# A hybrid decoder block: engine order pinned at the first seam of its Strassen MLP, other buffers at the second, one shared sum folded in a chunk earlier

## The chip, the cores and the metric

One core of a Trainium2 chip. The time is the device time of one execution in microseconds (us); the span is the part of it that the profile records, from the first instruction to the last. The engines are TensorE (PE, with its weight loads as PEld), VectorE (DVE), ScalarE (ACT), GpSimd (POOL) and SyncE (SP), which here only issues DMAs. All times of engines are from one profiled execution.

## The reference

One pre-norm layer on 1024 tokens of width 1024, in float32: a mixer (a state-space scan and an attention side by side), then an MLP with a squared ReLU, then a last norm. The change lies in the MLP:

```python
h = h + hybrid_mixer(rmsnorm(h, norm_mix_w), ...)
u = square(relu(rmsnorm(h, norm_mlp_w) @ w_up))      # 1024 x 4096
h = h + u @ w_down                                    # 1024 x 1024
return rmsnorm(h, norm_final_w)
```

## The kernel before

Matmuls have float32 quality by splitting: each operand is a high part, a rounded copy, and a low part, the rest; a product is the sum high x high, high x low and low x high, so three matmuls for each k-tile. `parts(o, src, by)` makes both: ScalarE copies the high part, the engine `by` (mostly VectorE) subtracts it to get the low part.

Both matmuls of the MLP are done by a seven-product Strassen scheme on 2 x 2 blocks. Up-projection: 16 pairs of 256 columns of `w_up`. One product of a pair is 12 matmuls of 512 columns into one bank (`up_mm`). The right operands b11, b21, b22, t1 to t4 (tiles `g_...`, four k-tiles each) are made once from the normalised rows and used by all pairs; the left ones (a11, s1, ...) are made for each pair by `up_split`: a sum on GpSimd, then `parts` (tiles `us_s`, `uo_...`). Results pass a bank a, b or c, go through ReLU and square, are summed by four GpSimd operations to the left operands of the down-projection (tiles `uc`), and are stored to DRAM (`uc_d`) by SyncE. Down-projection: 8 chunks of two pairs, in each 4 slots i (token rows i and i+4 of 128); a slot is seven products of 6 matmuls (`down_mm`), whose results VectorE adds to the rows `h1b`, read back from DRAM. Product a is used twice: its second form, the shared sum, is collected over the chunks in `acc`, and in the last chunk GpSimd adds `acc` to three halves of the rows (line 1546). `down_split` makes the right operands of a pair (tiles `do_...`), `down_in` loads and splits the left ones of a slot (tiles `ui`), two slots ahead. `final` norms and stores a row block.

The first seam is the way from the mixer's output projection (`oproj_jobs`, products `po`) into pairs 0 and 1. From the fourth row block on (`row`, line 1371) work for the MLP is placed after a number of matmuls (`after`): `left` (transposes `nt_l`) makes b11 and b21, `right_turn` and `right_sums` the sums `ta` (in `cc` lies a scaled copy). `norm_row` squares a row block on ScalarE, takes its root on GpSimd (`v_m`), and scales it on VectorE (`hn`). After the last `po`, lines 1387 to 1427 write the two pairs out step by step. The second seam is the way from the last two pairs (`tails`, 14 and 15) into chunk 0.

The order of instructions on each engine is chosen by the framework's scheduler: it takes program order as priority, but lets ready instructions go ahead. An engine whose key stands in `kept` has its instructions pinned in program order; before the change that is TensorE alone ("t") at the first seam, and none later. Buffers have tags with a fixed count (`BUFS`, `PBUFS` for banks); a tile waits until a buffer of its tag is free. On the way through the code: tags d, s, t and v are banks (2, 3, 2, 1); `hT`, `q`, `p`, `w`, `ws`, `v`, `t` and `p0` are SBUF buffers.

Of the kernel before, what the change touches and what calls it, by code (L numbers as in the profile page):

```python
# [45 lines left out]
def tile_hymba_block(  # L46
# [1238 lines left out]
    class Up:  # L1285
# [50 lines left out]
        def p7(self):  # L1336
            self.half = self.t1
            self.third(self.prod("b", "s3", "t3"))

        def p5(self):  # L1340
            self.half = self.t1
            self.third(self.prod("c", "s1", "t1"))

        def p4(self):
            b = self.prod("b", "a22", "t4")
# [5 lines left out]
        def p3(self):  # L1351
            c = self.prod("c", "s4", "b22")
            u2 = self.u2
            ve.tensor_tensor(out=u2, in0=c, in1=u2, op=ALU.add)
# [8 lines left out]
            for j in range(3):  # L1363
                sy.dma_start(out=d[:, :, 2 * j:2 * j + 2, :], in_=self.st[j])
            sy.dma_start(out=d[:, :, 6, :], in_=a22)

    OP = {"p1": "a11", "p2": "a12", "p6": "s2", "p7": "s3", "p5": "s1", "p4": "a22", "p3": "s4"}
    ups = {}
# [18 lines left out]
    for p in range(2):  # L1387
        ups[p] = Up(p, "dts")
    ups[0].p1()
    ups[1].p1()  # L1390
    for k in range(HK):
        right_turn(k, 1)
    for k in range(HK):
        right_sums(k, 1)
        parts(gtile("t2", k), ta[k][:, 1, :], ve)
    ups[0].p2()
# [237 lines left out]
```

## Time and profile before

| | us |
|---|---|
| median of 3 runs (1702.18 to 1708.83) | 1706.76 |
| the profiled execution's own time | 1701.5 |
| its span | 1699.7 |
| TensorE busy | 1614.2 |
| VectorE busy | 1113.4 |
| ScalarE busy | 821.6 |
| GpSimd busy | 803.6 |

The page is read from the engine with the largest share: where TensorE is busy all the time, other engines cost nothing; where it pauses, the bracket of the timeline names what it waited for. A pause also has an after-effect, which shows in the granted clock of a stretch and in longer matmuls behind it. Stages: mixer up to 1011, first seam 1011 to 1085, steady pairs to 1318, second seam to 1404, steady chunks to 1642, last chunk and end to 1699.7.

### The profile page before, as it was taken

What the parts mean: (1) busy time and instruction counts of PE and PEld (TensorE: products, weight loads), DVE (VectorE), ACT (ScalarE), POOL (GpSimd) and SP (SyncE); (2) the same over time, 40 slices, a digit from 0 to 9 for tenths busy, and PEclk for the clock granted to TensorE, in tenths of its full rate; (3) what the DMA queues carried; (4) which work ended last, traced back from release to release, by engine and by line L of the source; (5) the groups of instructions that cost most, each with busy time, mean ns of one, the idle gap of its engine ahead of it and who ended that gap; (6) DMA issues with size and microseconds to landing.
All of it is one profiled execution on the core that took longest, in us unless ns stands there. A gap on an engine that the chain in (4) does not pass through costs nothing.

```text
span 1699.7 us, 23561 instructions
## 1 busy us (share of the span) xinstructions
PE 1614.2 (95%) x7994; PEld 1341.5 (79%) x7994; DVE 1113.4 (66%) x2074; ACT 821.6 (48%) x1778; POOL 803.6 (47%) x873
## 2 busy tenths in 40 slices
PE   7999898899999999999999998999999969999996
PEld 7977687778888888888788876788888758888884
DVE  5666775667777677767874537755555646777754
ACT  4223443435565555555631126555445546666643
POOL 4242452454334334434320122655545678777757
PEclk9999899999999999999999999999999989999998
DMA  5122434431120211111442331354554675454432
GB/s 179 38 54 62 93 89 88 103 77 42 36 48 21 48 37 37 36 33 48 134 145 88 100 112 62 119 173 149 160 162 130 206 241 169 141 160 156 147 99 108
DMA packets 180288, 175.41 MB, mean 103 GB/s; under 512 B 44388, under 2 KB 153144, under 8 KB 180168
## 3 DMA queue, kind: packets, MB, share of 16 engines
q1 hardware_dynamic: 179000, 173.12, 34.9%
q8 instruction: 63, 1.03, 0.3%
q0 software_dynamic: 1024, 0.53, 0.1%
q14 instruction: 57, 0.47, 0.1%
q10 hardware_dynamic: 144, 0.26, 0.0%
HBM read 127.15 MB, written 46.73 MB: 102 GB/s over the span
## 4 chain that ended last, share of the span: by engine, by line
PE 69%; DVE 7%; DMA 7%; POOL 6%; ACT 4%; issue 4%; SPq 0%; POOLq 0%; DVEq 0%; ACTq 0%
PE po L85 9%; PE pj_qk L85 9%; PE pu_b L85 6%; PE pj_v L85 5%; DMA eb<-cum_d 5%; PE pn_a L85 4%; PE pu_c L85 4%; PE pn_b L85 4%; PE pn_c L85 4%; PE pu_a L85 4%; PE s L85 4%; PE o L85 4%; PE tp L85 3%; PE pj_x L85 3%; PE pn_d L85 2%
## 5 line engine op out<-in xcount | busy, mean ns | idle before, releaser
L85 POOL TENSOR_SCALAR p<-p,rs 128x512 f32<-128x512 f32 (+2 forms) x144 | 103.3, 722 | 246.6 <-DVE rs L85 133.5
L85 POOL TENSOR_TENSOR ui<-ui 128x384 fp32r<-128x384 f32 (+1 forms) x128 | 145.9, 1161 | 64.9 <-ACT ui L85 51.2
L85 PE MATMUL po<-wh_o,yy 128*128 128x512 f32 x512 | 163.9, 396 | 1.2 <-DVE k L85 1.2
L85 ACT ACTIVATE p<-s,mx 128x512 f32<-128x512 f32 (+1 forms) x192 | 110.4, 579 | 89.8 <-DVE mx L85 69.6
L85 DVE TENSOR_TENSOR pl<-tp,ph 128x512 fp32r<-128x512 f32 x192 | 106.0, 553 | 38.8 <-ACT ph L85 35.9
L85 ACT CAST ph<-tp 128x512 fp32r<-128x512 f32 x192 | 91.7, 478 | 70.1 <-PE tp L85 67.6
L85 ACT CAST ui<-ui 128x384 fp32r<-128x384 f32 (+1 forms) x128 | 71.5, 566 | 104.2 <-DMA ui<-uc_d 102.6
L85 PEld LDWEIGHTS po<-wh_o,yy 128*128 128x128 f32 x512 | 95.5, 189 | 19.7 <-DVE k L85 1.5
L85 PE MATMUL pj_qk<-hh,wl_qk 128*128 128x512 f32 x256 | 106.4, 416 | 0.0
L85 PE MATMUL pj_qk<-hl,wh_qk 128*128 128x512 f32 x256 | 106.3, 415 | 0.0
L85 PE MATMUL pj_qk<-hh,wh_qk 128*128 128x512 f32 x256 | 103.9, 406 | 0.0
L85 PE MATMUL s<-k,q 68*128 68x512 f32 (+7 forms) x384 | 101.9, 347 | 1.0 <-ACT p L85 0.7
L85 PE MATMUL po<-wl_o,yy 128*128 128x512 f32 x256 | 101.6, 397 | 0.0
L85 PE MATMUL pu_b<-g_t,uo_s 128*128 128x512 f32 x384 | 95.9, 400 | 5.0 <-DVE g_t L85 2.9
L85 PE MATMUL pn_c<-do_t,ui 128*128 128x512 f32 x384 | 97.8, 390 | 0.8 <-DVE h1b L85 0.8
L85 PE MATMUL tp<-ident,p 128*128 128x128 f32 x576 | 95.2, 273 | 1.2 <-POOL p L85 1.2
L85 PEld LDWEIGHTS pu_b<-g_t,uo_s 128*128 128x128 f32 x384 | 73.9, 193 | 22.6 <-DVE g_t L85 4.1
L85 PE MATMUL pz<-wh_z,hh 128*128 128x256 f32 (+1 forms) x256 | 77.4, 302 | 15.0 <-DVE z L85 10.9
L85 PE MATMUL pu_a<-g_b,uo_a 128*128 128x512 f32 x384 | 91.6, 389 | 0.0
L85 PEld LDWEIGHTS tp<-ident,p 128*128 128x128 f32 x576 | 72.7, 140 | 19.9 <-POOL p L85 2.6
L85 PEld LDWEIGHTS s<-k,q 128*128 128x128 f32 (+1 forms) x384 | 70.8, 188 | 20.2 <-ACT p L85 4.8
L85 PEld LDWEIGHTS pn_c<-do_t,ui 128*128 128x128 f32 x384 | 71.9, 188 | 16.6 <-DVE h1b L85 1.6
(290 smaller groups left out, 4520.0 us busy)
## 6 DMA issues: line engine op xcount, KB each, us to landing
uc_d<-uc SPq DMA_DIRECT2D x48, 512.0 KB, 3.2
ws_up<-in_w_up_dram SPq DMA_DIRECT2D x32, 512.0 KB, 3.7
wsd<-in_w_down_dram SPq DMA_DIRECT2D x32, 512.0 KB, 4.1
ui<-uc_d SPq DMA_DIRECT2D x64, 256.0 KB, 2.8
ui<-uc_d SPq DMA_DIRECT2D x64, 192.0 KB, 2.4
eb<-cum_d SPq DMA_DIRECT2D x16, 512.0 KB, 8.7
ws_qk<-in_w_in_dram SPq DMA_DIRECT2D x32, 256.0 KB, 3.4
wso<-in_w_out_dram SPq DMA_DIRECT2D x16, 512.0 KB, 3.4
```

The source lines that it names most:

```text
L85: i = call(*args, **kw)
```

## The change

Seven edits.

- First seam, order. From the fourth row block on GpSimd is pinned; after the last `po`, TensorE, VectorE, ScalarE and GpSimd are all pinned until the third product's matmuls are issued. The products are split in a part for TensorE (`m1` ...) and a part that reads the bank (`r1` ...), and the steps are written out in a new order. TensorE's own order stays.
- First seam, t4. Its high part is made by GpSimd rather than ScalarE, right after its sum, and all twelve operations on it are ahead of the second making of s1 on GpSimd. Two of the four k-tiles of b22 are made later. The transposes of the right side come two matmuls later.
- Second seam, homes. The left operands of slots 0 and 1 go to tag `q` (slot 1 was in `p`), those of slot 2 partly to `p` (were in `ws`); the rows of `h1b` go to `hT`, `q`, `q`, `p` (all were in `q`); in the ring of the right operands two `ws` take the place of two `hT`.
- Second seam, sums. The eight GpSimd sums and eight stores of pairs 14 and 15 are written after the loads for slots 0 and 1, no longer before `down_split`.
- Second seam, splits. The right operands of pairs 0 and 1 are split like all others: ScalarE makes a second copy in a bank (tag v), and VectorE subtracts that.
- Second seam, bank. The second product of slot 0 takes a bank of tag s instead of t.
- Shared sum. `acc` is added to the three halves by GpSimd in chunk seven (c = 6); in the eighth VectorE adds the bank itself to the three halves.

```diff
-                ve.tensor_tensor(out=self.u3, in0=bank, in1=self.half, op=ALU.add)
+                ve.tensor_tensor(out=self.u3, in0=bank, in1=self.t1, op=ALU.add)
...
         if dh == 1 and tt == 3:
+            kept.add("g")
             for p in range(2):
                 up_load(p)
...
             for k in range(HK):
-                after(72 + 5 * k, lambda k=k: (right_turn(k, 0), right_sums(k, 0)))
+                after(74 + 5 * k, lambda k=k: (right_turn(k, 0), right_sums(k, 0)))
...
+    kept.update("tvag")
+    u0, u1 = pair = [Up(p, "dts") for p in range(2)]
...
+    def third_sum(k):
+        tb[k] = sb("t", [P, 512], F32, f"tb{k}_3")
+        ve.scalar_tensor_tensor(
+            out=tb[k], in0=p22[k], scalar=mlpw(k + HK), in1=cc[k][:, 0, :], op0=ALU.mult, op1=ALU.subtract
+        )
+        parts(gtile("t3", k), tb[k], ve)
+
+    def fourth_sum(k):
+        tb[k] = sb("t", [P, 512], F32, f"tb{k}_4")
+        gp.tensor_tensor(out=tb[k], in0=cc[k][:, 1, :], in1=ta[k][:, 1, :], op=ALU.subtract)
+        o = gtile("t4", k)
+        gp.tensor_scalar(out=o[:, 0], in0=tb[k], scalar1=1.0, scalar2=1.0, op0=ALU.mult, op1=ALU.mult)
+        gp.tensor_tensor(out=o[:, 1], in0=tb[k], in1=r32(o[:, 0]), op=ALU.subtract)
+
+    u0.m1()
+    u0.r1()
+    u1.m1()
+    up_split(0, "s3", True)
+    u1.r1()
     for k in range(HK):
-        quarter("b22", k, p22[k], mlpw(k + HK))
...
+        right_turn(k, 1)
+    up_split(1, "s3", True)
+    u0.m2()
+    u1.m2()
     for k in range(HK):
...
+        right_sums(k, 1)
+        parts(gtile("t2", k), ta[k][:, 1, :], ve)
+    u0.r2()
+    u0.m6()
+    u1.m6()
+    third_sum(0)
+    third_sum(1)
+    u1.r2()
+    u0.r6()
+    third_sum(2)
+    third_sum(3)
+    u1.r6()
+    u0.m7()
+    u1.m7()
+    for k in range(HK):
+        fourth_sum(k)
+    for k in range(2):
+        parts(gtile("t1", k), ta[k][:, 0, :], ve)
+        quarter("b22", k, p22[k], mlpw(HK + k))
+    up_split(0, "s1", True)
+    for k in range(2, HK):
+        parts(gtile("t1", k), ta[k][:, 0, :], ve)
+    up_split(1, "s1", True)
+    u0.m5()
+    u1.m5()
+    u0.r7()
+    u1.r7()
+    up_split(0, "a22", True)
+    u0.r5()
+    up_split(1, "a22", True)
+    u1.r5()
+    quarter("b22", 2, p22[2], mlpw(HK + 2))
+    quarter("b22", 3, p22[3], mlpw(HK + 3))
+    u0.m4()
+    u1.m4()
...
+    kept.clear()
+    kept.add("t")
+    u0.r3()
+    u1.r3()
+    u0.sums()
+    u1.sums()
+    kept.clear()
...
-    wring = ["hT"] * 14 + ["w"] * 6 + ["hT"] * 2
-    uring = ["q"] * 4 + ["p"] * 4 + ["ws"] * 2
+    wring = ["hT"] * 14 + ["w"] * 6 + ["ws"] * 2
+    uring = ["q"] * 8 + ["p"] * 2
...
-            if p < CP:
-                parts(o, src[m], ve)
-            else:
...
-                hb = ps("s", f"hb_{m}_{p}")
...
+            hb = ps("v" if p < CP else "s", f"hb_{m}_{p}")
+            ac.copy(hb.bitcast(F32R), src[m])
+            ac.copy(o[:, 0], src[m])
+            ve.tensor_tensor(out=o[:, 1], in0=src[m], in1=hb, op=ALU.subtract)
...
-        bb = ps("t", f"pn_b{nm}")
+        bb = ps("t" if c or i else "s", f"pn_b{nm}")
...
-        else:
+        elif not last:
             read(ba, acc[i])
+        if c == NCH - 2:
+            for dst in (h22, h12, h21):
+                gp.tensor_tensor(out=dst, in0=dst, in1=acc[i], op=ALU.add)
         if last:
             for dst in (h22, h12, h21):
-                gp.tensor_tensor(out=dst, in0=dst, in1=acc[i], op=ALU.add)
+                read(ba, dst)
...
+        if i == 2:
+            for u in tails:
+                u.sums()
         for tt in (i, i + 4):
-            h1[tt] = sb("q", [P, D], F32, f"h1b_{tt}")
+            h1[tt] = sb(("hT", "q", "q", "p")[i], [P, D], F32, f"h1b_{tt}")
```

## Rows read from the trace of the kernel before

**Rows 1.** The page's first part, busy time and its share of the span and the instructions of each engine, over the whole execution.

```profile
PE 1614.2 (95%) x7994; PEld 1341.5 (79%) x7994; DVE 1113.4 (66%) x2074; ACT 821.6 (48%) x1778; POOL 803.6 (47%) x873
```

**Rows 2.** Busy time by stretch (from and to in us, length, then busy time and instructions of PE, PEld, DVE, ACT and POOL, TensorE's granted clock, the share of the DMA engines and GB/s): the steady pairs of the up-projection, then the two 20 us stretches of the second seam.

```profile
1085.00:1300.00 215.00, 215.00 (x951) 178.01 (x950) 124.97 (x148) 110.26 (x183) 115.67 (x82) 1.00 0.50 156
...
1340.00:1360.00 20.00, 17.93 (x80) 14.51 (x78) 15.99 (x20) 13.45 (x25) 13.63 (x10) 1.00 0.87 298
...
1360.00:1380.00 20.00, 8.76 (x36) 6.60 (x36) 10.32 (x16) 10.47 (x20) 15.57 (x13) 0.83 0.50 161
```

**Rows 3.** The timeline of TensorE at the first seam (start, length, engine, line, operation, out<-in, tile and form, count, and in brackets the idle time before it and what ended it).

```profile
1021.84 1.11 PE L85 MATMUL nt_l<-ident,hn 128*128 128x128 f32 x4 [3.90 <-ACT cc L85]
...
1040.48 5.61 PE L85 MATMUL pu_a<-g_b,uo_a 128*128 128x512 f32 x24
...
1061.08 0.50 PE L85 MATMUL pu_b<-g_t,uo_s 128*128 128x512 f32 x1 [2.09 <-ACT g_t L85]
...
1062.34 4.10 PE L85 MATMUL pu_b<-g_t,uo_s 128*128 128x512 f32 x9 [0.76 <-DVE g_t L85]
...
1068.60 5.08 PE L85 MATMUL pu_b<-g_t,uo_s 128*128 128x512 f32 x14 [2.16 <-DVE g_t L85]
...
1073.51 5.62 PE L85 MATMUL pu_c<-g_t,uo_s 128*128 128x512 f32 x24
```

**Rows 4.** The timelines of ScalarE, GpSimd and VectorE (columns as in group 3) in the last microseconds of TensorE's pause before 1021.84.

```profile
1014.17 1.05 ACT L85 ACTIVATE hn<-h 128x1024 f32<-128x1024 f32 x1
...
1016.56 0.19 POOL L85 TENSOR_SCALAR v_m<-ss_m 128x1 f32<-128x1 f32 x1
...
1016.83 1.29 POOL L85 TENSOR_TENSOR us_s<-ws_up 128x512 f32<-128x512 f32 x1
...
1018.08 0.55 POOL L85 TENSOR_TENSOR v_m<-v_m,mhalf 128x1 f32<-128x1 f32 x1
...
1018.66 1.74 DVE L85 TENSOR_SCALAR hn<-h,v_m 128x1024 f32<-128x1024 f32 x1 [3.68 <-POOL v_m L85]
```

**Rows 5.** The timelines of GpSimd and VectorE where the operands t2 and t3 are made at the first seam (g_t is their tile, ta and tb their sums).

```profile
1053.62 1.29 POOL L85 TENSOR_TENSOR us_s<-ws_up,ws_up 128x512 f32<-128x512 f32 x1 [4.29 <-DVE uo_s L85]
...
1049.80 0.87 DVE L85 SCALAR_TENSOR_TENSOR ta<-nt_r,prm,ta 128x256 f32<-128x256 f32 x2
...
1053.89 2.78 DVE L85 TENSOR_TENSOR g_t<-ta,g_t 128x512 fp32r<-128x512 f32 x3 [0.35 <-ACT g_t L85]
...
1057.19 1.28 DVE L85 TENSOR_TENSOR g_t<-ta,g_t 128x512 fp32r<-128x512 f32 x2
...
1059.63 2.06 DVE L85 SCALAR_TENSOR_TENSOR tb<-nt_r,prm,cc 128x512 f32<-128x512 f32 x3
...
1067.86 0.68 DVE L85 TENSOR_TENSOR g_t<-tb,g_t 128x512 fp32r<-128x512 f32 x1
```

**Rows 6.** The timeline of TensorE at the second seam; the third and fourth line are the start of slot 1, the last is the start of slot 3.

```profile
1360.57 1.66 PE L85 MATMUL pn_b<-do_t,ui 128*128 128x512 f32 x6 [2.64 <-DVE uu L85]
...
1365.01 1.66 PE L85 MATMUL pn_a<-do_t,ui 128*128 128x512 f32 x6 [1.42 <-DVE h1b L85]
...
1382.08 3.44 PE L85 MATMUL pn_a<-do_b,ui 128*128 128x512 f32 x6 [11.34 <-ACT ui L85]
...
1385.32 2.19 PE L85 MATMUL pn_b<-do_t,ui 128*128 128x512 f32 x6
...
1404.12 1.65 PE L85 MATMUL pn_a<-do_b,ui 128*128 128x512 f32 x6 [0.26 <-ACT acc L85]
```

**Rows 7.** The timelines of GpSimd (first and last sum of the last two pairs), SyncE's queue, ScalarE and VectorE at the second seam.

```profile
1363.62 1.28 POOL L85 TENSOR_TENSOR uc<-uc,uu 128x512 f32<-128x512 f32 x1
...
1375.17 1.26 POOL L85 TENSOR_TENSOR uc<-uc,uc 128x512 f32<-128x512 f32 x1
...
1366.18 10.79 SPq L85 DMA_DIRECT2D uc_d<-uc  x6
...
1377.08 2.85 SPq L85 DMA_DIRECT2D ui<-uc_d  x4
...
1334.51 0.62 ACT L85 CAST do_b<-wsd 128x512 fp32r<-128x512 f32 x1 [3.23 <-DMA wsd<-in_w_down_dram]
...
1363.06 0.58 ACT L85 CAST hb_t<-ds_t 128x512 fp32r<-128x512 f32 x1
...
1363.67 0.69 DVE L85 TENSOR_TENSOR do_t<-ds_t,hb_t 128x512 fp32r<-128x512 f32 x1 [0.35 <-ACT hb_t L85]
```

**Rows 8.** The page's sixth part, DMA issues (count, KB each, median us from issue to landing).

```profile
uc_d<-uc SPq DMA_DIRECT2D x48, 512.0 KB, 3.2
...
ui<-uc_d SPq DMA_DIRECT2D x64, 256.0 KB, 2.8
```

**Rows 9.** Busy time by stretch (columns as in group 2): the four slots of the seventh chunk.

```profile
1604.20:1642.30 38.10, 38.10 (x170) 31.55 (x169) 26.32 (x41) 22.04 (x42) 22.33 (x20) 1.00 0.36 112
```

**Rows 10.** The timelines of TensorE (first and last product of the eighth chunk), GpSimd and VectorE.

```profile
1642.26 1.52 PE L85 MATMUL pn_a<-do_b,ui 128*128 128x512 f32 x6
...
1686.99 1.54 PE L85 MATMUL pn_c<-do_t,ui 128*128 128x512 f32 x6
...
1686.91 3.75 POOL L85 TENSOR_TENSOR h1b<-h1b,acc 128x512 f32<-128x512 f32 x3 [0.73 <-DVE acc L85]
...
1689.47 0.69 DVE L85 TENSOR_TENSOR h1b<-h1b,pn_b 128x512 f32<-128x512 f32 x1 [2.04 <-POOL h1b L85]
```

More of the change, by code (lines that the diff above doesn't have):

```diff
@@ L1334, in third, with m7, r7, m5 @@
                 ac.activation(self.u3, self.u3, AF.Square)
[L1336 to L1345, printed above, removed]
+        def m7(self):
+            self.prod("b", "s3", "t3")
+        def r7(self):
+            self.third(self.bank["b"])
+        def m5(self):
+            self.prod("c", "s1", "t1")
+        def r5(self):
+            self.third(self.bank["c"])
+        def m4(self):
+            self.prod("b", "a22", "t4")
+        def r4(self):
             v = self.view("a12")
-            ve.tensor_tensor(out=v, in0=v3(b), in1=v3(self.t1), op=ALU.add)
+            ve.tensor_tensor(out=v, in0=v3(self.bank["b"]), in1=v3(self.t1), op=ALU.add)
             ac.activation(v, v, AF.Relu)
             ac.activation(v, v, AF.Square)
-        def p3(self):
-            c = self.prod("c", "s4", "b22")
+        def m3(self):
+            self.prod("c", "s4", "b22")
+        def r3(self):
             u2 = self.u2
-            ve.tensor_tensor(out=u2, in0=c, in1=u2, op=ALU.add)
+            ve.tensor_tensor(out=u2, in0=self.bank["c"], in1=u2, op=ALU.add)
             ac.activation(u2, u2, AF.Relu)
             ac.activation(u2, u2, AF.Square)
-            a21, a22, view = v3(u2), v3(self.u3), self.view
+        def sums(self, by=None):
+            a21, a22, view = v3(self.u2), v3(self.u3), self.view
             gp.tensor_tensor(out=view("s3"), in0=view("a11"), in1=a21, op=ALU.subtract)
@@ L1363, in p3, with step @@
             for j in range(3):
[L1364 to L1368, printed above, removed]
+                (by or sy).dma_start(out=d[:, :, 2 * j:2 * j + 2, :], in_=self.st[j])
+            (by or sy).dma_start(out=d[:, :, 6, :], in_=a22)
+        def step(self, n):
+            getattr(self, f"m{n}")()
+            getattr(self, f"r{n}")()
+            if n == 3:
+                self.sums()
+    OP = {1: "a11", 2: "a12", 6: "s2", 7: "s3", 5: "s1", 4: "a22", 3: "s4"}
     def row(tt, dh):
@@ L1386, in tile_hymba_block, with hi, lo @@
     drain()
[L1387 to L1396, printed above, removed]
-    ups[1].p2()
-    ups[0].p6()
-    ups[1].p6()
-    tb = {}
-    for k in range(HK):
+    kept.update("tvag")
+    u0, u1 = pair = [Up(p, "dts") for p in range(2)]
+    tb = {}
+    def hi(m, k, src):
+        ac.copy(gtile(m, k)[:, 0], src)
+    def lo(m, k, src):
+        o = gq[m][k]
+        ve.tensor_tensor(out=o[:, 1], in0=src, in1=r32(o[:, 0]), op=ALU.subtract)
+    def third_sum(k):
         tb[k] = sb("t", [P, 512], F32, f"tb{k}_3")
@@ L1432, in tile_hymba_block @@
         u = Up(p)
-        for m in ("p1", "p6", "p2", "p7", "p5", "p4", "p3"):
-            up_split(p, OP[m])
-            getattr(u, m)()
+        for n in (1, 6, 2, 7, 5, 4, 3):
+            up_split(p, OP[n])
+            u.step(n)
     tails = [Up(p) for p in (NPAIR - 2, NPAIR - 1)]
@@ L1438, in tile_hymba_block @@
         up_load(u.p)
-    for m in ("p1", "p2", "p6", "p5", "p7", "p4", "p3"):
+    for n in (1, 2, 6, 5, 7, 4, 3):
         for u in tails:
-            up_split(u.p, OP[m], True)
+            up_split(u.p, OP[n], True)
         for u in tails:
-            getattr(u, m)()
+            getattr(u, f"m{n}")()
+            getattr(u, f"r{n}")()
     CP = 2
```

47 lines of the change are left out of this document (18 added, 29 removed).

## The prediction, written before the change was run

> **What bounds the kernel now.** I read the busy shares first: TensorE works 95% of the span, the next engine 66% [rows 1], so only stretches in which TensorE pauses can be shortened. Then the table by stretch: in the steady pairs TensorE is busy 215.0 of 215 us at full clock, one matmul of 512 columns every 0.226 us (215/951), in the seventh chunk 38.10 of 38.10 [rows 2, 9]. Nothing is to be had there. So I went through TensorE's timeline for brackets. There are three places.
>
> First seam: a pause of 3.90 us while it waits for ScalarE's copy `cc`, and three of 2.09, 0.76 and 2.16 us ahead of the seventh product, for t3 [rows 3]. Behind them matmuls are stretched: 9 take 4.10 us, 14 take 5.08 us, where 8 and 13 steps of 0.226 and a last 0.39 would be 2.2 and 3.3 [rows 3]. Second seam: 2.64, 1.42 and 11.34 us [rows 6], with a granted clock of 0.83 in that stretch [rows 2]. Last chunk: the first product starts at 1642.26, the last ends at 1686.99 + 6 x 0.226 = 1688.35, so four slots take 46.1 us against 38.1 in the chunk before [rows 9, 10]; then 11.3 us to the span's end at 1699.7.
>
> All sums are made against the profiled execution (1701.5, span 1699.7). The median of the runs is 1706.76, 1.0031 times that; the result is carried over by this ratio.
>
> **First seam, the pause of 3.90.** The chain behind it: ScalarE's square of row block 4 ends at 1014.17 + 1.05 = 1015.2; GpSimd takes it up only at 1016.56, since it is busy with sums of the weights, and puts another (1.29 us) between the two steps of `v_m`; VectorE's scaling of the rows waits until 1018.66 and takes 1.74 us beside GpSimd; the split of b21, in line behind it, and ScalarE's copy follow [rows 4]. These sums, for s2 and s3, are written later than `v_m`; pinned, GpSimd can't hoist them. Then `v_m` goes at 1015.4 and ends 0.27 + 0.55 later, and scaling starts at 1016.3: 2.4 us earlier, and about 1 shorter. TensorE pauses 0.5 instead of 3.9. What the matmuls behind the pause lose I put at 1.2, an estimate from the 1.9 and 1.8 us that the two groups above lose (4.10 against 2.2, 5.08 against 3.3). Together +4.6, bounds 2.4 and 5.1. The sums that are no longer hoisted have until the second operand is split, long after; the two ticks by which the right side's transposes move are two matmuls (0.45 us) of the same TensorE work, nothing.
>
> **First seam, the written order.** TensorE's order doesn't change, so I count what it waits for, from E = 1040.48, the end of `po`; sixteen transposes after m1 end at E + 7.1. Before: the last part of t3 is ready at 1067.86 + 0.68 = E + 28.1, the seventh products end at 1073.51 = E + 33.0, and there is no pause after [rows 3, 5]. Written out, VectorE can't go ahead any more: for each k-tile of t2 it does two sums (0.87 for the two), waits for ScalarE's cast (0.58 [rows 7], and two hand-overs of 0.05), then subtracts (0.60): 2.2 to 2.3, four times, E + 16.4. For t3 a sum of 0.67, a cast, a subtraction: 2.05, four times, and one bank read (0.60) between: E + 25.3. The subtraction has two SBUF operands, and where a GpSimd sum runs it waits: three of them took 2.78 us with a sum of 1.29 that had begun before them, though two alone take 1.28 [rows 5]; a lost 0.9. In the new order GpSimd has twelve operations for t4 in a row from E + 8 on (eight of 1.29 as in the row, four copies that take no more: 13 to 15 us), so seven of the eight subtractions have one beside them. I charge half a sum, 0.6, to each: +4.2, E + 29.5. After that come r6, two k-tiles of t1, two of b22 and s1 (six of about 0.63), and the fifth product starts at E + 33.6 against E + 33.0. A value of -1.0 with the hand-overs. Bounds: no collision is 4.2 earlier (+2.8), a full sum of 1.25 at each is 4.5 later (-5.5). GpSimd's sums for s1, queued behind t4, are done by E + 27 or so, before VectorE gets to them. First seam: 4.6 - 1.0 = **+3.6**.
>
> Here a rule speaks against the change. The Trainium skill, SBUF — State Buffer, section "SBUF: two separate sides", says that VectorE with two SBUF inputs and GpSimd share a port pair by an exclusive lock, held for a whole instruction, while the other fully blocks. The 2.78 us agree with that. Taken strictly, each of the seven could lose a whole operation; this is the -5.5 above, and rival A.
>
> **Second seam.** Slot 0 starts at 1356.4 and ends at 1370.7 instead of 1365.9; slot 1 starts at 1382.08, slot 3 at 1404.12 [rows 6]. The 2.64 is the bank in t that still holds a product of pair 14; a bank of tag s is free, so it goes. The 1.42 (VectorE late with a read) I keep: slot 0 ends at 1367.3. The 11.34: slot 1's `ui` tiles live in `p`, where the results of pairs 14 and 15 stay until they are stored; their GpSimd sums run from 1363.62 to 1376.4, the stores follow on SyncE's queue until 1377, and the `ui` loads stand behind them at 1377.08 [rows 7]. In `q` they are free before slot 0 starts, since t4's last product is issued before that, so slot 1 runs on at once, to 1367.3 + 9.5 = 1376.8. What is late next is slot 2: two of its tiles wait for `p` now. The last of the sums that such a store needs ends at 1375.1 if the sums run as before; store 3.2, load 2.8 [rows 8], cast 0.6, subtraction 1.3: 1383.0. So a pause of 6.2 stays, and its stretched matmuls: after 11.34 they cost 3.44 + 2.19 - 2 x 1.54 = 2.5 [rows 6], taken again. Slot 3 starts at 1383.0 + 9.5 + 2.5 = 1395.0: **+9.1**. Bounds: without the pause 1386.3 (+17.8); slot 1 still held on SyncE's queue, only the bank's gain (+2.6). Added: 14 copies by ScalarE of 0.58, 8.1 us in a stretch where it is busy 13.45 of 20 [rows 2, 7]; it has the room, and the subtraction has one SBUF operand fewer.
>
> **Shared sum.** In the last chunk VectorE waits for GpSimd's three adds (3.75 us) in every slot, and the last slot's second read waits 2.04 us for them [rows 10]. Three bank reads by VectorE (0.69 each) take their place: it has time for them. Of the 8.0 us lost I keep 1.0 for the norms; in chunk seven GpSimd is busy 22.3 of 38.1 [rows 9], so twelve adds (15.2) fit, with 1.0 lost in the first slot, where other sums are queued. The end moves as the second read does, from 1689.47 to about 1687.2, +2.2. Together **+8.2**, bounds +1 and +10.
>
> Splitting each step in two functions and `half` change no instruction: nothing.
>
> **Sum.** 3.6 + 9.1 + 8.2 = 20.9; 1701.5 - 20.9 = 1680.6, times 1.0031 = **1686**.
>
> **The rivals.**
> A. The collisions at the first seam cost the whole 5.5: the seam gives nothing, 16.4 in all, 1690. For it: seven subtractions beside twelve GpSimd operations. Against: the lock goes to whoever starts first, so not each one loses all.
> B. SyncE's queue, which isn't pinned, still has the stores ahead of slot 1's loads: second seam +2.6, 14.4 in all, 1692. For it: program order is only a priority there. Against: the buffers are free before 1356.4, and the stores end 20 us later.
> C. The fold moves the stalls to chunk seven: tail +1, 1693. For it: `h1b` is read by the same VectorE there. Against: GpSimd's 15 free us.
> D. The change does little of what it says: two of the three places stay as they are, a gain of some 8, 1699.
> S. Slower: the copies of pairs 0 and 1 go through the one bank of tag v, one after another, each a ScalarE copy and a VectorE subtraction. They begin at 1334.5 [rows 7]; at 0.58 + 0.69 and hand-overs, 1.4 each, the 14 are done at 1354. If ScalarE or VectorE stand in between for reads of pairs 14 and 15, a round may take long: 5.5 us would put the last at 1411.5, slot 3 at 1430.5, 26.4 later than now, and 1721 in all. It decides from 2.0 us a round (slot 0's last products want the last operands at 1362), and is slower by over 0.5% from 5.1. Against: a later split of this kind runs from 1363.06 to 1364.36, 1.3 us [rows 7].
>
> **How the numbers follow.** Forecast 0.42, A 0.16, B 0.14, C 0.08, D 0.13, S 0.07. About 0.5% is what a measurement of this kernel can tell from no change: 1698.2 to 1715.3. So faster 0.42 + 0.16 + 0.14 + 0.08 = 0.80, same 0.13, slower 0.07. The range runs from 1675 (all three terms half-way to their better bounds: 5.8, 13.5 and 9.1 are 28 in the trace; 3 more for the unknown sizes) to 1701, which takes in A to C and most of D, and leaves out S.
>
> **What would show it.** Right: no bracket above 1 us on the `nt_l` products; the last part of t3 between E + 25 and E + 30; slot 1 right behind slot 0, one pause of 4 to 8 us before slot 2; no GpSimd `h1b` in the last chunk, which takes 39 to 40 us. Wrong: pauses ahead of the fifth product (s1 late on GpSimd), slot 0 stretched by waits for do tiles, brackets in chunk seven.

## The result and the profile after

| | before | after |
|---|---|---|
| median, us (range, runs) | 1705.48 (1702.18 to 1708.83, 4) | 1721.24 (1719.21 to 1723.99, 4) |
| ratio, 95% interval | | 1.0093 (1.0067 to 1.012) |
| profiled execution, span | 1699.7 | 1718.1 |

The kernel became slower by 0.9%. The forecast was 20 us faster. By TensorE's timeline in the two profiled executions the 18.4 us of span lie as follows (E is again the start of the first product of pair 0). The marks are, before, 1040.48 and 1073.51 [rows 3], 1089.85 (pair 2) and 1356.41 (slot 0), 1642.26 and 1688.53, where the last matmul ends (1686.99 + 1.54) [rows 10]; after, 1040.25, 1079.07, 1099.62, 1376.94 (1378.22 less the 1.28 waited), 1665.47 and 1707.23:

| stage | before | after | difference |
|---|---|---|---|
| span's start to E | 1040.48 | 1040.25 | -0.2 |
| E to the fifth product | 33.03 | 38.82 | +5.8 |
| fifth product to pair 2 | 16.34 | 20.55 | +4.2 |
| pair 2 to the end of pair 15 | 266.56 | 277.32 | +10.8 |
| end of pair 15 to the last chunk | 285.85 | 288.53 | +2.7 |
| last chunk | 46.27 | 41.76 | -4.5 |
| last matmul to the span's end | 11.17 | 10.87 | -0.3 |

The first fence is TensorE's timeline after, from the fourth row block to pair 2 (start, length, engine, line, operation, tiles, shape, count, and in brackets the idle time before it and its releaser).

```profile
1019.51 0.66 PE L85 MATMUL nt_l<-ident,hn 128*128 128x128 f32 x4 [0.45 <-ACT cc L85]
...
1029.29 0.50 PE L85 MATMUL po<-wh_o,yy 128*128 128x512 f32 x1 [1.10 <-DVE h L85]
...
1037.89 0.66 PE L85 MATMUL nt_r<-ident,hn 128*128 128x128 f32 x4 [2.42 <-ACT cc L85]
...
1079.07 8.15 PE L85 MATMUL pu_c<-g_t,uo_s 128*128 128x512 f32 x24 [7.14 <-ACT uo_s L85]
1099.62 2.88 PE L85 MATMUL pu_a<-g_b,uo_a 128*128 128x512 f32 x12
1102.34 2.88 PE L85 MATMUL pu_b<-g_t,uo_s 128*128 128x512 f32 x12
...
1115.35 5.49 PE L85 MATMUL pu_b<-g_t,uo_s 128*128 128x512 f32 x12 [7.41 <-DVE uu L85]
```

The pause of 3.90 us [rows 3] is down to 0.45, as forecast, but 1.10 and 2.42 have come in its place, so E moves by 0.2 only. A pause of 7.14 stands before the fifth product, where there was none, and 24 matmuls behind it take 8.15 us in place of 5.62 [rows 3]. And in pair 2, in what was a stretch without pauses [rows 2], TensorE waits 7.41 for a bank read by VectorE, and 12 matmuls then take 5.49 against 2.88.

The other engines there, after: ScalarE's cast of s2, GpSimd's run for t4 with s1 behind it, ScalarE at the right operands, VectorE.

```profile
1035.53 0.62 ACT L85 CAST uo_s<-us_s 128x512 fp32r<-128x512 f32 x1 [3.54 <-POOL us_s L85]
...
1059.22 1.29 POOL L85 TENSOR_TENSOR tb<-cc,ta 128x512 f32<-128x512 f32 x1 [13.17 <-DVE g_t L85]
...
1073.38 1.26 POOL L85 TENSOR_TENSOR tb<-cc,ta 128x512 f32<-128x512 f32 x1
...
1076.65 2.95 POOL L85 TENSOR_TENSOR us_s<-ws_up,ws_up 128x512 f32<-128x512 f32 x2
...
1074.67 0.69 ACT L85 ACTIVATE g_b<-nt_r,prm 128x512 fp32r<-128x512 f32 x1 [8.08 <-POOL tb L85]
...
1078.39 0.62 ACT L85 CAST uo_s<-us_s 128x512 fp32r<-128x512 f32 x1 [0.43 <-POOL us_s L85]
...
1063.06 1.70 DVE L85 TENSOR_TENSOR g_t<-tb,g_t 128x512 fp32r<-128x512 f32 x1 [0.69 <-ACT g_t L85]
...
1075.39 0.75 DVE L85 SCALAR_TENSOR_TENSOR g_b<-nt_r,prm,g_b 128x512 fp32r<-128x512 f32 x1 [7.40 <-ACT g_b L85]
```

GpSimd begins t4 at 1059.22, which is E + 19 and not E + 8: by the bracket its first sum needs a buffer of tag t that VectorE's first subtraction for t3 gives free. Its run has a gap too: it stands 3.93 us before t4's second copy (1068.14), for which the trace names no releaser. Its last sum begins at 1073.38, and only when that is done does ScalarE make b22's first copy, after standing for 8.08 us; VectorE then stands 7.40 for that copy. s1's sums come last, at 1076.65, and s1's first cast waits for them until 1078.39.

Pair 2 after: SyncE's loads of the weights, GpSimd, VectorE (the product whose bank is read is the one at 1102.34 above).

```profile
1078.39 8.31 SPq L85 DMA_DIRECT2D ws_up<-in_w_up_dram  x3
...
1110.44 1.26 POOL L85 TENSOR_TENSOR uc<-uu,uu 128x512 f32<-128x512 f32 x1
1111.66 1.26 POOL L85 TENSOR_TENSOR us_s<-us_s,ws_up 128x512 f32<-128x512 f32 x1
...
1112.95 1.75 DVE L85 TENSOR_TENSOR us_s<-ws_up,us_s 128x512 f32<-128x512 f32 x1 [4.81 <-POOL us_s L85]
1114.62 0.68 DVE L85 TENSOR_TENSOR uu<-pu_b,ut 128x512 f32<-128x512 f32 x1
```

The same steps before, with that product first:

```profile
1092.57 2.88 PE L85 MATMUL pu_b<-g_t,uo_s 128*128 128x512 f32 x12
...
1046.62 32.83 SPq L85 DMA_DIRECT2D ws_up<-in_w_up_dram  x5
...
1086.15 1.29 POOL L85 TENSOR_TENSOR us_s<-us_s,ws_up 128x512 f32<-128x512 f32 x1 [3.76 <-DVE uo_s L85]
...
1090.00 1.30 POOL L85 TENSOR_TENSOR uc<-uc,uu 128x512 f32<-128x512 f32 x1
...
1095.02 1.61 DVE L85 TENSOR_TENSOR us_s<-ws_up,us_s 128x512 f32<-128x512 f32 x1
1096.55 0.68 DVE L85 TENSOR_TENSOR uu<-pu_b,ut 128x512 f32<-128x512 f32 x1
```

VectorE's order is the same in both: the sum s4 of pair 3 (`us_s`) stands ahead of pair 2's bank read (`uu<-pu_b`). s4 needs GpSimd's s2 of pair 3. Before, that is done at 1087.4, ahead of the sums (`uc`) of pairs 0 and 1; after, it stands between them and is done at 1112.9, 7.7 us after the end of the product that the read takes (1102.34 + 2.88). The first load of pair 2's weights goes out at 1046.62 before and at 1078.39 after.

The second seam after, TensorE, GpSimd and SyncE's queue:

```profile
1378.22 0.73 PE L85 MATMUL pn_a<-do_b,ui 128*128 128x512 f32 x2 [1.28 <-ACT ui L85]
...
1382.35 1.65 PE L85 MATMUL pn_a<-do_b,ui 128*128 128x512 f32 x3 [2.94 <-POOL ui L85]
...
1400.38 1.65 PE L85 MATMUL pn_b<-do_t,ui 128*128 128x512 f32 x3 [11.18 <-POOL ui L85]
...
1383.49 1.29 POOL L85 TENSOR_TENSOR ui<-ui 128x512 fp32r<-128x512 f32 x1
1384.73 1.29 POOL L85 TENSOR_TENSOR uc<-uc 128x512 f32<-128x512 f32 x1
...
1393.36 1.28 POOL L85 TENSOR_TENSOR uc<-uc,uc 128x512 f32<-128x512 f32 x1
...
1397.16 3.16 POOL L85 TENSOR_TENSOR ui<-ui 128x384 fp32r<-128x384 f32 x3
...
1364.05 2.36 SPq L85 DMA_DIRECT2D ui<-uc_d  x4
...
1369.97 2.02 SPq L85 DMA_DIRECT2D ui<-uc_d  x4
```

The loads for slots 0 and 1 now go out before slot 0 starts. But the pause of 11.34 [rows 6] is one of 11.18, and it has moved into slot 0: four of its seven products stand behind it. It is now GpSimd's splits of `ui` that end it, at 1397.16, behind the sums `uc` that began at 1377 and end at 1394.6.

The last chunk after, first the windows (length, then busy time of TensorE, its weight loads, VectorE, ScalarE and GpSimd, the granted clock, the DMA share and GB/s), then the timeline of TensorE and VectorE around a pause.

```profile
1665.50:1707.30 41.80, 39.21 (x169) 31.01 (x167) 29.23 (x43) 16.14 (x38) 26.92 (x35) 1.00 0.36 120
```

```profile
1690.40 1.66 PE L85 MATMUL pn_a<-do_t,ui 128*128 128x512 f32 x6 [1.65 <-DVE h1b L85]
...
1688.99 0.75 DVE L85 SCALAR_TENSOR_TENSOR fsq<-h1b,v_f,wfb 128x512 f32<-128x512 f32 x1 [3.19 <-POOL v_f L85]
1689.66 0.68 DVE L85 TENSOR_TENSOR h1b<-h1b,pn_a 128x512 f32<-128x512 f32 x1
```

GpSimd's adds of `acc` are in the chunk before; only the last of them run on into this one, to 1666.7. What is left are pauses of 1.65, 0.72 and 0.15: the norm's scaling waits 3.19 us for GpSimd's `v_f`, and the bank read stands behind it.

### The profile page after: what moved, and what is told of

The parts are those of the page before. It is cut to its first block, busy times and chain, and to the rows that moved or that the text cites. A ratio compares the mean times of both kernels' runs of the same rounds, so it can differ in the third digit from the quotient of the medians.

```text
span 1718.1 us, 23618 instructions
## 1 busy us (share of the span) xinstructions
PE 1618.2 (94%) x7994; PEld 1343.8 (78%) x7994; DVE 1118.8 (65%) x2082; ACT 826.1 (48%) x1788; POOL 803.7 (47%) x877
## 4 chain that ended last, share of the span: by engine, by line
PE 67%; DMA 8%; DVE 6%; issue 5%; ACT 5%; POOL 5%; SPq 0%; POOLq 0%; DVEq 0%; ACTq 0%
PE po L85 9%; PE pj_qk L85 8%; PE pu_b L85 6%; PE pj_v L85 5%; DMA eb<-cum_d 5%; PE pu_a L85 4%; PE pu_c L85 4%; PE pn_a L85 4%; PE pn_b L85 4%; PE pn_c L85 4%; PE s L85 4%; PE o L85 4%; PE tp L85 3%; PE pj_x L85 3%; PE pn_d L85 2%
## 5 line engine op out<-in xcount | busy, mean ns | idle before, releaser
L85 DVE TENSOR_TENSOR uo_s<-us_s,uo_s 128x512 fp32r<-128x512 f32 x64 | 56.5, 884 | 46.9 <-ACT uo_s L85 46.6
```

What stands on the lines that cost most here:

```text
L85: i = call(*args, **kw)
```

## The experiments

All times are in us, ratios are to the kernel before on the same chip with 95% intervals. The runs come from several chips, so runs are compared by their ratios and by their traces. The three columns on the right are from the profiled executions, counted from E, because E itself differs by up to 8 us between executions of kernels that hardly differ up to there.

| run | median | ratio | fifth product | pair 2 | end of pair 15 |
|---|---|---|---|---|---|
| before | 1703.0 to 1705.5 | 1 | 33.0 | 49.4 | 315.9 |
| after | 1721.2 | 1.0093 | 38.8 | 59.4 | 336.7 |
| e1 first seam alone | 1723.9 | 1.0115 (1.010 to 1.013) | 38.8 | 59.0 | 335.3 |
| e2 second seam alone | 1705.8 | 1.0004 (0.9993 to 1.0016) | 33.0 | 49.4 | 316.1 |
| e3 fold alone | 1700.1 | 0.9975 (0.9963 to 0.9986) | 33.0 | 49.4 | 315.9 |
| e4 s1's sums first | 1721.0 | 1.0099 (1.0084 to 1.0114) | 39.1 | 59.2 | 335.9 |
| e5 t4's parts late | 1712.4 | 1.0048 (1.0031 to 1.0066) | 29.4 | 50.8 | 327.2 |
| e6 s4 on GpSimd | 1715.4 | 1.0067 (1.0049 to 1.0085) | 38.8 | 59.3 | 329.9 |
| e9 both | 1710.1 | 1.0038 (1.0025 to 1.0051) | 29.4 | 50.8 | 325.2 |
| e10 TensorE alone pinned | 1703.7 | 1.0000 (0.9988 to 1.0012) | 32.4 | 51.1 | 317.8 |
| e15 without GpSimd's pin | 1715.3 | 1.0067 (1.0049 to 1.0086) | 34.1 | 53.1 | 329.6 |
| e16 GpSimd pinned | 1703.8 | 0.9998 (0.9985 to 1.0011) | 33.6 | 52.9 | 319.6 |
| e18 ScalarE pinned | 1705.3 | 1.0005 (0.9994 to 1.0015) | 31.7 | 50.9 | 320.2 |
| e13 order free, t4 late, fold | 1695.3 | 0.9956 (0.9940 to 0.9972) | 25.3 | 43.0 | 311.0 |

**The parts alone.** e1 is the kernel before with the first seam's edits, e2 with the second seam's, e3 with the fold.

> The kernel before with the first seam's edits alone. Theory 1 (the loss is made at the first seam: GpSimd's twelve pinned operations for t4 wait for VectorE's t3 and stand ahead of the sums for s1, TensorE pauses 7 us before the fifth product, and as much again is lost in pairs 2 and 3, whose sums queue behind those of pairs 0 and 1): the whole loss and the part that the fold gave back, so about 20 us slower than before, 1725. Theory 2 (the second seam costs what the whole lost, since each split of pairs 0 and 1 passes one bank): near the kernel before, 1706 or less. Theory 3 (the seam costs only the 10 us up to pair 2; the rest comes by chance of the scheduler's order): about 1716.

> The kernel before with the second seam's four edits alone (homes, late sums, splits through a bank, bank of slot 0). Theory 1: within 4 us of before, 1703 to 1710, since the scheduler puts GpSimd's sums ahead of the splits of ui in any case. Theory 2: slower by 10 us or more, 1717. The prediction's own reckoning: 9 us faster, 1697.

> The kernel before with the shared sum folded in at chunk seven alone. From the trace of the changed kernel, in which the last chunk takes 41.6 us in place of 46.1 and the end 11.0 in place of 11.3: 4.8 us faster, 1701. The prediction's own reckoning: 8.2 faster, 1698. If chunk seven takes on the stalls in place of the last: 0 to 1 faster.

Measured 1723.9, 1705.8 and 1700.1. The first seam makes all of the loss, and makes it before pair 3 is done: behind pair 2's pause (7.47 us in e1) there is none up to the second seam. The second seam gives nothing; the fold gains 0.25%. For each of the three the theory named first holds.

**Which order at the first seam.** e4 writes s1's sums ahead of t4 (`s1_sum` makes such a sum alone, in a tile `us_s1b`), e5 moves t4's copies and subtractions (and its claims on tag q) behind s1, e6 gives pair 3's s4 to GpSimd, e9 is e5 and e6.

```diff
+++ e4
+    s1_sum(0)
+    s1_sum(1)
     for k in range(HK):
         fourth_sum(k)
+++ e5
     up_split(1, "s1", True)
+    for k in range(HK):
+        fourth_parts(k)
     u0.m5()
+++ e6
-            add("s4", a12, ops["s2"], ALU.subtract, gp if thrift else ve, ops["s2"] if thrift else None)
+            add("s4", a12, ops["s2"], ALU.subtract, gp if thrift or p == 3 else ve, ops["s2"] if thrift else None)
```

> The changed kernel with GpSimd's two sums for s1 written ahead of its twelve operations for t4; the rest of the seam, and all pins, as they are. Theory 1: the pause of 7.1 us before the fifth product goes or falls under 2 us, since the sums read only the weights; if the pause alone is what GpSimd's order costs, 5 to 8 us faster than the changed kernel, 1713 to 1716; if pairs 2 and 3 recover as well, 1705. If ScalarE's casts of t3 and t1 set the fifth product and not the sums: unchanged, 1721.

> The changed kernel with GpSimd's twelve operations for t4 parted: the four sums stay where they are, the four copies and four subtractions come after s1 (and so do the buffers of tag q that t4 takes). All pins stay. Theory 1a (b22's first tile waits for the buffer that the fourth of t4's sums gives free, and that sum stands behind t4's other operations): the sums end soon after t3, ScalarE's stand of 8 us at b22 goes, the fifth product's pause falls from 7 us to under 2, and the kernel is 5 to 8 us faster than the changed one, 1713 to 1716. Theory 1b (pinning VectorE and ScalarE makes the wait, whatever stands there): the pause stays above 5 us, 1720.

> The changed kernel with the sum s4 of pair 3 made by GpSimd in place of VectorE; nothing else. Theory 1 (pair 2's pause of 7.4 us comes from this one sum: it waits on VectorE for GpSimd's s2 of pair 3, which is queued behind the sums of pairs 0 and 1, and pair 2's bank read stands behind it): the pause goes, with its stretched matmuls about 10 us, 1711. Theory 2 (another operation of GpSimd's late queue takes the place): a pause of 4 to 7 us stays, 1716 to 1721.

> The changed kernel with both mends together: t4's copies and subtractions behind s1 (alone 9 us faster than the changed kernel), and the sum s4 of pair 3 on GpSimd (alone 6 faster). Theory 1 (two separate places): the gains add up, 15 us, 1706, which is the kernel before; what then stays is the rest of the seam's loss, the fold's gain having been in all the time. Theory 2 (the second pause is a consequence of the lateness of the first): less than the sum, 1709 to 1712.

e4 gained nothing, and it corrected the theory. GpSimd, ScalarE and TensorE in it, then ScalarE and GpSimd in e5:

```profile
1050.42 1.30 POOL L85 TENSOR_TENSOR us_s1b<-ws_up,ws_up 128x512 f32<-128x512 f32 x1 [0.63 <-DVE uo_s L85]
...
1076.00 1.26 POOL L85 TENSOR_TENSOR tb<-cc,ta 128x512 f32<-128x512 f32 x1
...
1077.29 0.69 ACT L85 ACTIVATE g_b<-nt_r,prm 128x512 fp32r<-128x512 f32 x1 [8.09 <-POOL tb L85]
...
1081.14 1.22 PE L85 MATMUL pu_c<-g_t,uo_s 128*128 128x512 f32 x2 [8.06 <-ACT uo_s L85]
```

```profile
1068.28 0.68 ACT L85 ACTIVATE g_b<-nt_r,prm 128x512 fp32r<-128x512 f32 x1
...
1068.72 1.29 POOL L85 TENSOR_TENSOR tb<-cc,ta 128x512 f32<-128x512 f32 x1 [0.75 <-DVE g_t L85]
```

In e4 s1's sums are done at 1051.7, 29 us before they are wanted, and the pause is longer (8.06). ScalarE's copy for b22 begins at 1077.29, when t4's last sum (1076.00 + 1.26) is done; s1's cast stands behind it. The copy reads nothing of t4, so what it waits for is a buffer: it was the claims on tag q, and s1's sums alone change nothing. e5 bears that out: with t4's claims behind b22's, the copy begins at 1068.28, before t4's last sum (1068.72), and the fifth product starts at E + 29.4 with pauses of 0.17 and 0.85. By the ratios the kernel gains 0.45% over the changed one. (e5 moves GpSimd's work for t4 too; how much of the gain is the claims' alone wasn't measured.) e6 takes the pause of 7.41 in pair 2 away (0.90, 1.40 and 0.67 are left) and gains 0.26%. By the end of pair 15 in the traces e5 gains 9.5 us, e6 6.8, both together 11.5 and not 16.3: in e9 pauses of 1.69 and 2.85 stay in pairs 2 and 3. Theory 2 of e9 was the better one, and 1710 was still slower than before.

**Which pin.** e10 keeps the written order, homes and fold and pins TensorE alone; e15 adds ScalarE's and VectorE's pins, e16 GpSimd's (from the fourth row block on, as in the change), e18 ScalarE's.

```diff
+++ e10, e15, e18
-            kept.add("g")
+++ e10
-    kept.update("tvag")
+++ e15
-    kept.update("tvag")
+    kept.update("tva")
+++ e16
-    kept.update("tvag")
+    kept.update("tg")
+++ e18
-    kept.update("tvag")
+    kept.update("ta")
```

> The changed kernel with its written order, its homes and its fold, but nothing pinned at the first seam beyond TensorE, as in the kernel before. The scheduler is free to bring s1 and pair 3's sums ahead. Theory 1 (the order of claims on the buffers of tag q, t4 before b22, makes the wait, pinned or not): ScalarE still stands before b22 until t4's last sum, a pause of 3 to 7 us before the fifth product, 1708 to 1716. Theory 2 (the pins make it): no pause over 2 us there, and the kernel is at the fold's gain, 1700 to 1704.

> The changed kernel with GpSimd free at the first seam (and from the fourth row block on), VectorE and ScalarE pinned as they were. Theory 1 (ScalarE's and VectorE's pins make the 7 us before the fifth product, GpSimd's pin those of pairs 2 and 3): the pause of 7 us stays, pair 2's of 7.4 goes, 1709 to 1712. Theory 2 (GpSimd's pin makes both): 1701 to 1705. Theory 3 (it makes neither): 1719 to 1722.

> The changed kernel with VectorE and ScalarE free at the first seam and GpSimd pinned as it was. Theory 1: t1's and s1's casts go ahead of b22's copies, but s1's sums stand behind t4 on GpSimd, so that a pause of 5 to 7 us stays before the fifth product, and pairs 2 and 3 lose as in the changed kernel: 1717 to 1721. Theory 2 (the first pause needs ScalarE's pin, the second doesn't): 1709 to 1713.

> The changed kernel with ScalarE alone pinned at the first seam, VectorE and GpSimd free. Theory 1 (ScalarE's order does it: b22's first copy, which waits for t4's last sum, stands ahead of t1's and s1's casts, and VectorE only follows): a pause of 4 to 7 us before the fifth product and one in pair 2, 1713 to 1716, as with VectorE pinned too. Theory 2 (VectorE's pin does it): no pause in pair 2, 1703 to 1706.

e10 lies between its theories: a pause of 6.55 before the fifth product stays, as in theory 1, yet the kernel is 1.0000, as in theory 2. ScalarE, VectorE and TensorE in it:

```profile
1063.76 2.18 ACT L85 CAST g_t<-ta 128x512 fp32r<-128x512 f32 x4
...
1075.73 1.26 ACT L85 ACTIVATE g_b<-nt_r,prm 128x512 fp32r<-128x512 f32 x2 [0.80 <-POOL tb L85]
...
1071.12 5.12 DVE L85 TENSOR_TENSOR g_t<-ta,g_t 128x512 fp32r<-128x512 f32 x3
...
1080.83 7.99 PE L85 MATMUL pu_c<-g_t,uo_s 128*128 128x512 f32 x24 [6.55 <-DVE g_b L85]
```

ScalarE still waits at b22 for t4's sums (`g_b` at 1075.73). The pause's bracket names VectorE's half of b22: the fifth product's bank is of tag s, where the transposes lie from which b22 is made, so a late b22 holds TensorE by this way too. But all four casts of t1 have gone ahead (1063.76), and the seventh products have ended at E + 25.8 in place of 33.0, so that the fifth starts at E + 32.4, sooner than before, pause and all. Pairs 2 to 15 have no pause. Still, the fold alone is at 0.9975: as written in the change, and with nothing but TensorE pinned, the order takes back what the fold gives.

e15 and e18 differ by VectorE's pin alone, and on top of ScalarE's it costs 10 us (1.0067 against 1.0005), 7 of them behind pair 2's start. VectorE pinned without ScalarE wasn't run. In e15 VectorE waits as in the changed kernel:

```profile
1110.65 1.74 DVE L85 TENSOR_TENSOR us_s<-ws_up,us_s 128x512 f32<-128x512 f32 x1 [4.82 <-POOL us_s L85]
```

It is the same wait without GpSimd's pin, so theory 1 of e15, that GpSimd's pin makes pair 2's pause, is wrong; 1715 lies in none of the three ranges. e16, at 1703.8, is below both of its ranges; e18, at 1705.3, is where its theory 2 put it, with a pause of 6.52 before the fifth product all the same, and small ones in pairs 2 and 3 (0.59 and 1.39). How late pair 3's s2 is done against the end of the product whose read waits behind it, and the pause: before 8.0 us ahead, none (1087.44 against 1092.57 + 2.88); e10 8.0 ahead, none; e16 7.5 ahead, none; e18 0.4 late, 0.59; e15 7.7 late, 7.43; after 7.7 late, 7.41. So ScalarE's pin moves this sum by 8.4 us, up to the edge, and VectorE's by 7.3 more, past it. GpSimd's pin alone costs nothing in the whole.

**What the order is worth.** e13 is the kernel before with the fold and the written order, e5's place for t4, and TensorE alone pinned; e8 is the fold with GpSimd pinned from the fourth row block to E and s2's sums written earlier.

```diff
+++ e8
+            kept.add("g")
...
+            for p in range(2):
+                after(46 + 4 * p, lambda p=p: s2_sum(p))
```

> The kernel before with the fold and the first seam's written order, with nothing pinned there beyond TensorE and with t4's copies and subtractions behind s1. Theory 1 (the order is worth its earlier t3 once the waits are gone): the fifth product at 29 to 31 us behind the end of the output projection in place of 33.0, pair 2 up to 3 us earlier, 1697 to 1698 against 1700 for the fold alone. Theory 2 (the third and fourth products wait for t4 and b22 instead): 1700 to 1703.

> The kernel before with the fold, and GpSimd pinned from the fourth row block to the end of the output projection, with the sums for s2 of pairs 0 and 1 written 24 and 29 matmuls earlier, so that ScalarE doesn't wait for them; the written order after the output projection isn't taken. Theory 1 (the pause of 3.9 us on the transposes is really gained by the pin, and was given back by the late s2 sums): the output projection ends 3 to 5 us earlier, and the kernel is 3 to 5 us faster than the fold alone (1700), 1695 to 1697. Theory 2 (VectorE and ScalarE set that stretch, so the pause only comes elsewhere): within 1.5 us of 1700.

In e13 the fifth product follows the seventh without a pause, and pair 2 starts 6.4 earlier than before:

```profile
1069.47 5.84 PE L85 MATMUL pu_c<-g_t,uo_s 128*128 128x512 f32 x24
...
1087.18 2.88 PE L85 MATMUL pu_a<-g_b,uo_a 128*128 128x512 f32 x12
```

With the fold 1695.3: by the ratios the order gains 0.2% over e3, though the intervals overlap; by the trace the end of pair 15 comes 4.9 earlier, more than the 3 expected. e8: 1700.5, 0.9981 (0.9970 to 0.9992), as e3. Its pauses are 1.43 and 3.71 in place of e3's 3.75, 0.46 and 0.50; the second is again ScalarE's `cc` behind a cast of s2 that waits 3.58 us for GpSimd. Whether still earlier sums would free the 3.9 wasn't tried.

**The second seam.** e7 is e3 with the second seam's edits and GpSimd pinned over the `ui` splits and the sums; e11 takes the copies through the bank out of e7; e12 is e3 with slot 0's bank alone; e14 is e7 with four of the eight sums on VectorE.

```diff
+++ e7
+    kept.add("g")
     for i in range(4):
         if i < 2:
             down_in(0, i)
...
+    kept.clear()
+++ e14
+            by = ve if self.p >= NPAIR - 2 else gp
+            by.tensor_tensor(out=view("s3"), in0=view("a11"), in1=a21, op=ALU.subtract)
+            by.tensor_tensor(out=view("s1"), in0=a21, in1=a22, op=ALU.add)
```

> The kernel before with the fold and the second seam's four edits, and GpSimd pinned there, so that its subtractions for the left operands of slots 0 and 1 can't be passed by the sums of pairs 14 and 15. Theory 1 (the loads are early, as forecast, and only GpSimd's order takes the 9 us back): slot 1 follows slot 0 with no pause over 2 us, and the kernel is 6 to 10 us faster than the fold alone (1700), 1690 to 1694. Theory 2 (the pause only moves on, to slot 2, whose tiles wait for the stores of the sums): 1698 to 1702.

> The kernel before with the fold, the second seam's edits and GpSimd pinned there (1700), but with the right operands of pairs 0 and 1 split as before, without the second copy. Theory 1 (the 14 copies fill ScalarE from the last products of pair 14 until slot 0, so that the casts of ui come late): the pauses of 1.3 and 2.5 us at slot 0 go, 3 to 5 us faster, 1695 to 1697. Theory 2 (slot 2's loads and the reads of h1b set the end of this stretch in any case): 1698 to 1702.

> The kernel before with the fold and, of the second seam, only the bank of tag s for the second product of slot 0. The prediction's reckoning: the pause of 2.6 us goes, 1697.5. Rival: slot 0 ends earlier, but slot 1 starts when its loads come, so the pause of 11.3 us grows by as much: 1700.

> The kernel with fold, second seam and GpSimd pinned there (1700), with four of the eight sums of pairs 14 and 15 made by VectorE in place of GpSimd. Theory 1 (GpSimd's work, then stores, then loads set where slot 2 can start, in whatever order): the last sum ends some 5 us earlier, slot 2 starts 4 to 6 us earlier, 1694 to 1696. Theory 2 (VectorE's reads of h1b or ScalarE's copies set it): 1698 to 1702.

| run | median | ratio | end of pair 15 to last matmul |
|---|---|---|---|
| before | | 1 | 332.1 |
| e2 | 1705.8 | 1.0004 | 334.1 |
| e3 | 1700.1 | 0.9975 | 328.9 |
| e7 | 1699.8 | 0.9975 (0.9963 to 0.9987) | 329.0 |
| e11 | 1702.4 | 0.9987 (0.9978 to 0.9997) | 330.0 |
| e12 | 1701.1 | 0.9974 (0.9962 to 0.9986) | 328.4 |
| e14 | 1698.1 | 0.9971 (0.9958 to 0.9984) | 326.6 |

e7, the windows of 20 us (columns as above), and TensorE's later pauses with SyncE's queue:

```profile
1360.00:1380.00 20.00, 15.83 (x59) 11.91 (x59) 9.94 (x15) 13.14 (x26) 18.10 (x16) 0.91 0.60 224
1380.00:1400.00 20.00, 12.48 (x37) 8.74 (x35) 7.02 (x11) 11.08 (x21) 16.74 (x15) 0.77 0.85 292
1400.00:1420.00 20.00, 20.00 (x87) 16.49 (x86) 13.00 (x21) 14.13 (x28) 19.92 (x19) 0.97 0.62 211
```

```profile
1384.82 2.93 PE L85 MATMUL pn_a<-do_t,ui 128*128 128x512 f32 x6 [4.14 <-DVE h1b L85]
...
1397.48 0.95 PE L85 MATMUL pn_a<-do_b,ui 128*128 128x512 f32 x2 [3.38 <-ACT ui L85]
...
1378.27 11.49 SPq L85 DMA_DIRECT2D uc_d<-uc  x6
...
1391.47 5.71 SPq L85 DMA_DIRECT2D ui<-uc_d  x9
```

With GpSimd's order put right slot 1 does follow slot 0, but the sums now end at 1389, the last stores behind them, and slot 2's loads go out at 1391.47: the wait is at slot 2, and VectorE's reads of `h1b` are late by 4.14. The pauses add up to 11.6 (1.30, 2.52, 0.29, 4.14, 3.38) against 15.7 before (2.64, 1.42, 11.34, 0.26), and the time is the same. Theory 2 holds. In e12 the bank's pause goes and the next grows (12.81 in place of 11.66, and 1.83 in place of 1.39): the rival holds. e11 is no faster than e7, so the copies weren't the bound. In e14 the stretch is 2.4 shorter, half of what theory 1 expected; by the ratio alone it can't be told from e7. The ratios of e7 and e11 also carry something that isn't the second seam's: though nothing is edited there, their pair 2 starts at E + 50.6, 1.2 us later than in e3.

**A version faster than both.** e17 is e13 with e14's second seam.

> The free written order with t4 late and the fold (0.9956 of before), and in addition the second seam's edits with GpSimd pinned there and four of the eight sums on VectorE (which ended chunk 0 some 2 us earlier by the trace, 0.9971 with the fold alone at 0.9975). If the two add up: 1692 to 1694 where before is at 1704. If the second seam gives nothing in the mean of runs: 1695 to 1697.

1693.6 (1688.5 to 1695.3, 6 runs), ratio 0.9932 (0.9915 to 0.9949): 0.7% faster than before, 1.6% faster than the changed kernel. That is in the range given for both gains together; its interval overlaps e13's, and in the traces the stretch from pair 15 to the last matmul is only 1.0 shorter than e13's (326.9 against 327.9). So the second seam's share of it isn't shown.

## Why the prediction was wrong

**The first pause, +4.6 forecast, 0.2 measured.** The mechanism was right (3.90 to 0.45). The step that failed is "The sums that are no longer hoisted have until the second operand is split, long after". The split's cast on ScalarE stands ahead of the `cc` copies: it waits 3.54 us for s2 (1035.53), and TensorE waits for `cc`. I looked at when the sum is used and not at what is queued behind its user. e8 writes these sums earlier, and its pauses only move (1.43 and 3.71).

**The written order, -1.0 forecast, -5.8 measured up to the fifth product.** t3 was right: its last part is ready at 1066.10 + 0.69 = E + 26.5, forecast E + 25 to E + 30, and the seventh products end at E + 31.7 in place of 33.0. The collisions were few, since GpSimd started so late (one subtraction for t3 took 1.70 in place of 0.69, at 1063.06), so rival A was wrong. What failed is "In the new order GpSimd has twelve operations for t4 in a row from E + 8 on" and, with it, s1 "done by E + 27 or so". Neither looked at buffers: t4's sums need those that t3 gives free (E + 19), and b22 takes one that t4's last sum gives free. e4 and e5 show it. So the fifth product came at E + 38.8, not E + 33.6. I had named "pauses ahead of the fifth product (s1 late on GpSimd)" as a sign. It came, and s1 was late; but b22's buffer alone held as long (e4). (By the working's own figures the better bound, +2.8, should read 4.2 less 1.0, +3.2; nothing hangs on it.) In e4 ScalarE stood 8.09 us before one copy for b22, with the casts of t1 and of the finished s1 queued behind it. The Trainium skill (PSUM — Partial Sum Buffer, section "Engine vs sequencer instructions") says "ScalarE/VectorE/GpSimdE queues are strict FIFO", and the trace agrees.

**Behind the fifth product, nothing forecast, -15.0 measured (4.2 up to pair 2, 10.8 in the pairs).** This term was missing, and it is the largest. The working stopped at the fifth product, on the ground that steady pairs have no pauses. Part of the 4.2 is the stretch of 24 matmuls behind the pause (8.15 for 5.62). For the 10.8, the pins on ScalarE and VectorE together put pair 3's s2 late (the delays above), and e6 shows that the wait goes through s4 and the bank read behind it. Why the scheduler then puts that sum behind the others stays open. Late loads of the weights (1078.39 against 1046.62) aren't the reason by themselves: in e15 and e18 the first load goes out early (1050.32 and 1049.10) and the sum is late, in e16 it goes out late (1072.86) and the sum is early.

**The second seam, +9.1 forecast, -2.7 measured; alone, 0.** "In `q` they are free before slot 0 starts" was right for the loads. "so slot 1 runs on at once" failed: GpSimd's splits of `ui` stood behind the sums, and not even slot 0 ran through. And had they not (e7), the same sums would have come later and slot 2 with them: I took "the sums run as before" while the work that they had waited behind was to go first. My reading is that GpSimd's sums, then stores, then loads hold the stretch, whatever the order: in the trace only taking sums away shortened it (e14; by less in e17), by half of what was expected, and no ratio settles it. Of the rivals B came nearest in size, but not in place: the loads were early.

**The fold, +8.2 forecast, 4.8 in this trace, 0.25% alone.** The mechanism was right, the size off at two terms: the last chunk loses 3.7 over 38.1 and not 1.0, since the norm's scaling stands ahead of bank reads, and the end moves by 0.3 and not 2.2: the last store goes out 7.2 us behind the last matmul in place of 8.2, but the span ends 3.7 us behind that store in place of 3.0. Why the store takes longer stays open. Chunk seven has one pause of 0.51, so rival C was wrong.

Rival S gave 1721, close to the time, but by another mechanism: with the bank and no first seam (e2) the kernel is at 1.0004, and without the bank (e11) nothing is gained. Rival D had it that two of the three places stay as they are; so it was with the first pause and the second seam, but D had no place that loses.

## What to carry to other kernels

A written order is two things: who goes first, and who takes which buffer first. Follow each claim on a tag to the instruction that gives the buffer free, and then to all that is queued behind the claimant; here the order was worth nothing as first written (e10) and some 0.2% with t4's claims late (e13 against e3, intervals overlapping), and pins on the other engines cost 0.9%. Pin such engines only where a run shows a gain, and leave them to go round a wait: GpSimd's pin alone was free (e16), ScalarE's and VectorE's together cost 0.7% (e15). TensorE was pinned at the first seam in every run, so what its own pin is worth isn't shown. And where a pause is the end of a chain of work on another engine, as at the second seam, moving work in the chain moves the pause: count the engine's work, not the pause.
